# First norm per stream behind the X loads, last output banks in a fixed order, the last gate spread inside the mixer

## Chip, cores and metric

The kernel runs on one core of a Trainium2 chip. The metric is the device time of one execution in microseconds, the median of three executions. The engines of the core are TensorE (PE: matmuls, with its weight loads as PEld), VectorE (DVE), ScalarE (ACT), GpSimd (POOL) and SyncE (SP), which issues nearly all loads.

## The reference, cut to what matters

Two layers are applied to 256 latent tokens (x) and 256 context tokens (ctx), each of width 1024. The two streams share the weights and have their own shift, scale and gate (nine vectors for each layer, made from c and c_ctx).

```python
def rmsnorm(x, w):
    r = lax.rsqrt(jnp.mean(x32 * x32, axis=-1, keepdims=True) + EPS)
    return (x32 * r) * w

def trunk_layer(xl, xc, ml, mc, ...):
    xl = xl + 0.5 * g1l * swiglu(modulate(rmsnorm(xl, norm_w[0]), sh1l, sc1l), w_ffn1_in, w_ffn1_out)
    # the same for xc
    hl = modulate(rmsnorm(xl, norm_w[1]), sh2l, sc2l)        # and hc
    mix_l, mix_c = token_mixer(hl, hc, w_in, ...)            # latent attention | gated conv, one output projection
    xl = xl + g2l * mix_l
    xl = xl + 0.5 * g3l * swiglu(modulate(rmsnorm(xl, norm_w[2]), sh3l, sc3l), w_ffn2_in, w_ffn2_out)
    # the same for xc, except behind the mixer of the last layer

for i in range(DEPTH):                                       # DEPTH = 2
    ml = split(silu(c) @ w_ada[i] + b_ada[i], 9)             # and mc from c_ctx
    xl, xc = trunk_layer(...)
return rmsnorm(xl, final_norm_w)
```

The output is the latent stream, 256 x 1024 in float32.

## The kernel before, in words

**Layout.** The residual stream lies transposed in SBUF as `X`: eight tiles (`kt` or `m`, 128 features each) of 512 columns, the 256 context tokens (s = 0) first and then the 256 latent tokens (s = 1). Every float32 product is made of three matmuls (`mm3`, L224 to L226) on a high and a low part of both operands. `wload` reads a weight tile of 128 x 1024 (512 KB), makes its high part on ACT (L216) and its low part on DVE or POOL (L220). It holds three raw slots and five slots for each part. The order of the instructions on every queue is laid out when the program is built, by a scheduler that plays the program through on modelled times; the order of the Python code is only the priority. `tc.issue_after(x)` binds instructions behind `x` on their own engine.

**Start (L702 to L740).** SP loads the condition vectors, then the first pair of modulation weights (`waf`, for `ct` = 0), then `norm_w` and `b_ada`, then `X` in four pieces of 512 KB. The first norm squares the pieces on ACT (L715), sums them over four feature tiles at a time with a strided DVE reduction (L716), and calls `rstd` once for both streams: column sums on PE (`psn_s`, L239), add epsilon on DVE (L242), the power -1/2 on POOL (L244), and a spread over the partitions on PE (`psn_r`, L247), copied to `R0` by ACT (L718). Then the loop over `ct` runs. For each of the eight feature tiles it makes the shift and scale of the first norm (`ada_first`: 128x32 matmuls `psa` on `waf`, L145, copy L148; `ada_first_end`: matmuls with `sel`, L153, and three small DVE operations into `first`). It then applies the norm (`Norm.apply`: `t` on DVE L296, high part `h` on ACT L297, low part on DVE L298, for each stream), and adds this tile's share to six products of the first feed-forward layer that are kept open at once (`early`, banks `mme`). `waf` has four slots for each of its two halves.

**Modulation.** The other 128 chunks of `w_ada` are multiplied and summed on DVE (`ada_chunk`, L173) beside the feed-forward products; `PACE` says how many go with each step of a feed-forward layer, and `ada_until` fetches at once what is still missing.

**The mixer (L480 to L699)** makes the projections, the keys and queries, and goes through the heads in a software pipeline, with convolution matmuls as filler. It ends with `into_x`, which adds the output projection to `X` (L343) and squares the new tiles for the next norm (`acc`, L275 and L279). In the last layer `Norm.ahead` also makes unnormed operands (`ax`, L265 and L266), on which the next two pairs of products (`psf`) start.

**The last feed-forward layer (`ffn_end`)** keeps the latent stream alone, and its second product has tokens in the rows. Four PSUM banks (`pse`: two token tiles `tt` by two halves `h` of the features) gather it over eleven steps `j`. Beside step 0, `prepare` spreads the gate over the partitions (L412, matmuls with the identity, copied to `gb` at L419) and transposes three of the four quarters of the latent `X` (L423, copied to `xt` at L425). The fourth quarter is added by matmuls into its bank (L434). `gb` multiplies the weights of the second product (L211). Behind the last step the first token tile's banks get steps 8 to 10 and then the second's; for each bank `xt` is added (L463), squared with a row sum (L464) and multiplied with the final weight (L466); for each token tile `v` (L471), a power on POOL (L473), two scalings (L474, L475) and two output DMAs (L477) follow.

## Time and profile before

| what | value |
|---|---|
| median of the three runs | 1670.31 us (1669.78 to 1673.23) |
| profiled execution, its own time | 1671.43 us |
| span of the profiled execution | 1669.6 us |
| mean granted TensorE clock | 0.994 |
| PE busy | 1631.2 us (98% of the span) |
| PEld busy | 1394.4 us (84%) |
| DVE busy | 1052.5 us (63%) |
| ACT busy | 624.7 us (37%) |
| POOL busy | 189.8 us (11%) |
| read from HBM | 246.28 MB, 148 GB/s over the span |

The busy time of PE overlaps from one matmul to the next, so the distance of two starts is what a matmul costs: 0.23 us for 512 columns and 0.12 us for 256 at the full clock. The column `PEclk` of a table by stages is the granted clock as a share of the full one. In a timeline the first number is the start, the second the duration (of the whole group where `xN` stands), and the brackets give the idle time of the engine before it and what ended that.

### The profile page before, as it was taken

Reading aid. Unit: us, or ns where it says so; the run is one execution under the profiler, and the core shown is the slowest. Engines: PE = TensorE matmul, PEld = TensorE weight load, DVE = VectorE, ACT = ScalarE, POOL = GpSimd, SP = SyncE. Lnnn points to the kernel's source line nnn. Section 1 sums busy time; section 2 is a strip of 40 time slices with the busy share of each in tenths; the row PEclk is TensorE's granted clock in tenths of the full one; section 3 lists DMA queues with packets and bytes.
Section 4 is the critical chain, followed back from the end, with each engine's and each line's share of the span. In section 5 each row is a group of like instructions: output and inputs, shape, how many; then the busy total and the mean of one; then the engine's idle time right before and its main releaser. Section 6 shows DMA issues by size and latency. Waiting matters only on the chain.

```text
span 1669.6 us, 22712 instructions
## 1 busy us (share of the span) xinstructions
PE 1631.2 (98%) x8885; PEld 1394.4 (84%) x8885; DVE 1052.5 (63%) x1695; ACT 624.7 (37%) x1010; POOL 189.8 (11%) x159
## 2 busy tenths in 40 slices
PE   6999999999999999999999999999999999999998
PEld 5888888889877788888888888888888988989997
DVE  5677777776577476556555576654445479776665
ACT  4422222324466443321332243322322357664443
POOL 0000000023111240000000330000000421430000
PEclk9999999999999999999999999999999999989999
DMA  9465555552222125444444334544444323446553
GB/s 376 146 203 191 191 186 178 178 190 75 76 74 77 51 89 177 139 152 152 140 150 151 101 124 157 174 158 160 162 157 146 110 90 126 152 141 200 190 173 118
DMA packets 73355, 249.59 MB, mean 149 GB/s; under 512 B 8736, under 2 KB 12960, under 8 KB 73248
## 3 DMA queue, kind: packets, MB, share of 16 engines
q1 hardware_dynamic: 72960, 247.62, 44.7%
q8 instruction: 70, 1.15, 0.3%
q10 hardware_dynamic: 288, 0.52, 0.1%
q14 instruction: 37, 0.30, 0.1%
HBM read 246.28 MB, written 1.05 MB: 148 GB/s over the span
## 4 chain that ended last, share of the span: by engine, by line
PE 91%; DVE 3%; ACT 1%; issue 1%; DMA 1%; POOL 1%; SPq 0%; POOLq 0%; DVEq 0%; ACTq 0%
PE mm L224 27%; PE mm L225 27%; PE mm L226 26%; PE pse L224 1%; PE pse L225 1%; PE pse L226 1%; PE pso L659 1%; PE pst L646 1%; POOL wlo L220 1%; DVE h L298 1%; PE mme L224 1%; PE mme L226 1%; PE mme L225 1%; DVE t L296 1%; PE psn_r L247 1%
## 5 line engine op out<-in xcount | busy, mean ns | idle before, releaser
L216 ACT CAST whi<-wraw 128x1024 fp32r<-128x1024 f32 x314 | 328.1, 1048 | 793.8 <-PE mm L225 448.1
L225 PE MATMUL mm<-h,whi 128*128 128x512 f32 (+1 forms) x1648 | 582.3, 355 | 4.9 <-DVE h L298 4.9
L224 PE MATMUL mm<-h,whi 128*128 128x512 f32 (+1 forms) x1648 | 581.5, 357 | 3.3 <-ACT h L297 3.3
L226 PE MATMUL mm<-h,wlo 128*128 128x512 f32 (+1 forms) x1648 | 580.5, 354 | 0.0
L220 DVE TENSOR_TENSOR wlo<-wraw,whi 128x1024 fp32r<-128x1024 f32 x258 | 317.6, 1233 | 156.1 <-ACT whi L216 147.9
L224 PEld LDWEIGHTS mm<-h,whi 128*128 128x128 f32 x1648 | 309.5, 189 | 53.5 <-issue 7.3
L225 PEld LDWEIGHTS mm<-h,whi 128*128 128x128 f32 x1648 | 311.8, 189 | 48.6 <-DVE h L298 7.0
L226 PEld LDWEIGHTS mm<-h,wlo 128*128 128x128 f32 x1648 | 311.6, 189 | 42.8
L173 DVE SCALAR_TENSOR_TENSOR junk<-wa,scb 128x1024 f32<-128x1024 f32 x224 | 272.4, 1248 | 31.2 <-DMA wa<-in_w_ada 30.8
L220 POOL TENSOR_TENSOR wlo<-wraw,whi 128x512 fp32r<-128x512 f32 x112 | 156.4, 1421 | 1123.7 <-ACT whi L216 822.5
L225 PE MATMUL mm<-hid,whi 128*128 128x512 f32 (+1 forms) x627 | 223.1, 356 | 0.0
L226 PE MATMUL mm<-hid,wlo 128*128 128x512 f32 (+1 forms) x627 | 222.9, 355 | 0.0
L224 PE MATMUL mm<-hid,whi 128*128 128x512 f32 (+1 forms) x627 | 222.1, 356 | 0.0
L383 DVE TENSOR_TENSOR sg<-sg,mm 128x512 f32<-128x512 f32 (+1 forms) x85 | 51.9, 611 | 156.3 <-PE mm L226 145.8
L225 PEld LDWEIGHTS mm<-hid,whi 128*128 128x128 f32 x627 | 118.5, 189 | 16.8
L224 PEld LDWEIGHTS mm<-hid,whi 128*128 128x128 f32 x627 | 118.5, 189 | 16.8
L226 PEld LDWEIGHTS mm<-hid,wlo 128*128 128x128 f32 x627 | 118.5, 189 | 16.8
L343 DVE SCALAR_TENSOR_TENSOR X<-mm,mod,X 128x256 f32<-128x256 f32 x120 | 53.4, 479 | 91.1 <-PE mm L226 90.3
L211 DVE TENSOR_TENSOR wraw<-wraw,gb 128x1024 f32<-128x1024 f32 x22 | 26.9, 1225 | 52.9 <-DMA wraw<-in_f2r 52.3
L230 DVE TENSOR_TENSOR hid<-sg,hid 128x512 fp32r<-128x512 f32 (+1 forms) x88 | 56.1, 638 | 0.5 <-ACT hid L229 0.5
L279 DVE TENSOR_TENSOR acc<-acc,sq 128x256 f32<-128x256 f32 x62 | 44.9, 745 | 15.4 <-ACT sq L275 15.3
L229 ACT CAST hid<-sg 128x512 fp32r<-128x512 f32 (+1 forms) x88 | 49.4, 563 | 12.0 <-DVE sg L383 12.0
(198 smaller groups left out, 1455.3 us busy)
## 6 DMA issues: line engine op xcount, KB each, us to landing
wa<-in_w_ada SPq DMA_DIRECT2D x128, 512.0 KB, 4.2
wraw<-in_f1i SPq DMA_DIRECT2D x88, 512.0 KB, 3.3
wraw<-in_f2i SPq DMA_DIRECT2D x88, 512.0 KB, 3.4
wraw<-in_f1o SPq DMA_DIRECT2D x44, 512.0 KB, 3.3
wraw<-in_w_in SPq DMA_DIRECT2D x32, 512.0 KB, 3.3
wraw<-in_f2o SPq DMA_DIRECT2D x22, 512.0 KB, 3.3
wraw<-in_f2r SPq DMA_DIRECT2D x22, 512.0 KB, 4.3
waf<-in_w_ada SPq DMA_DIRECT2D x16, 512.0 KB, 8.0
```

The lines of the kernel that those rows point to most:

```text
L173: nc.vector.scalar_tensor_tensor(junk, wt, 1.0, scb[:, s, :], ALU.mult, ALU.mult, accum_out=md[:, s, ct:ct + 1])
L211: nc.vector.tensor_tensor(raw, raw, by, ALU.mult)
L216: nc.scalar.copy(w[0], raw)
L220: eng.tensor_tensor(w[1][:, a:a + step], raw[:, a:a + step], f32(w[0][:, a:a + step]), ALU.subtract)
L224: nc.tensor.matmul(ps, w[0], x[0], start=start, stop=False)
L225: nc.tensor.matmul(ps, w[0], x[1], start=False, stop=False)
L226: return nc.tensor.matmul(ps, w[1], x[0], start=False, stop=stop)
L229: nc.scalar.copy(hi, src)
L230: return eng.tensor_tensor(lo, src, f32(hi), ALU.subtract)
L279: nc.vector.tensor_tensor(self.acc[s], self.acc[s], sq, ALU.add)
L343: end = nc.vector.scalar_tensor_tensor(xm, pt[:, s * T - c[0]:(s + 1) * T - c[0]], mod(d, gate, s, m), xm, ALU.mult, ALU.add)
L383: nc.vector.tensor_tensor(sg, sg, ps[1], ALU.mult)
```

## The change

- **Start.** The four pieces of `X` are loaded first, then `norm_w` and `b_ada`, then the first pair of `waf`. The first norm is made for each stream by itself (`first_rstd`): the strided reduction is replaced by additions of 128x512 and 128x256 on DVE, `rstd` is called once for each stream, and `ada_first(0)` stands between the two calls. Ahead of all this PE gets 40 transposes of the identity, whose result nobody reads (`WARM`), and POOL one power of 128x4.
- **The gate of the last layer** is spread in `mixer` (`spread`), between the heads and `into_x`, and its chunks are asked for there; `PACE` of the second layer's first feed-forward goes from 1.25 to 1.4.
- **The three transposed quarters** are made at steps 4, 5 and 6 of `ffn_end` (`turn_x`) and no longer at step 0; the matmuls that add the fourth quarter move from step 0 of its bank to step 1.
- **The last banks.** The remaining matmuls of the second token tile's banks are bound behind those of the bank before them.
- `wload` gets an argument `after`, which no call uses.

```diff
--- before.py
+++ after.py
@@ -50,13 +50,14 @@
 BURST = (5.0, 4.0)
 KEYS_AT = (0, 1)
 TAIL = 3
+WARM = 40
 NAHEAD = 2
 POOLED = 512
 EARLY = 6
 LEAD = 1
 EARLY_AT = (1, 1, 2, 2, 3, 3)
 NT1 = 3
-PACE = (1.75, 1.0, 1.25, 0.9)
+PACE = (1.75, 1.0, 1.4, 0.9)
 
 
 @with_exitstack
@@ -111,6 +112,14 @@
     nc.vector.tensor_copy(sel, ident[:, 0:2])
     for j in range(1, 4):
         nc.vector.tensor_tensor(sel, sel, ident[:, 32 * j:32 * j + 2], ALU.add)
+
+    warm = small.tile([P, 4], F32, tag="r", name="warm")
+    nc.gpsimd.memset(warm, 1.0)
+    nc.gpsimd.tensor_tensor(warm, warm, mhalf, ALU.pow)
+
+    warmed = psn.tile([P, TT], F32, tag="psn", name="psw")
+    for _ in range(WARM):
+        nc.tensor.transpose(warmed[:, 0:P], ident, ident)
 
 
     c_sb = const.tile([P, NKT, 2], F32, name="c_sb")
@@ -204,7 +213,7 @@
 
     turn, share = [0, 0], [0]
 
-    def wload(src, n, tags=("whi", "wlo"), by=None):
+    def wload(src, n, tags=("whi", "wlo"), by=None, after=None):
         raw = slot("wraw", "wraw")[:, :n]
         load(raw, src)
         if by is not None:
@@ -217,7 +226,8 @@
         step = POOLED if pooled else n
         for a in range(0, n, step):
             eng = nc.gpsimd if pooled else nc.vector
-            eng.tensor_tensor(w[1][:, a:a + step], raw[:, a:a + step], f32(w[0][:, a:a + step]), ALU.subtract)
+            with tc.issue_after(after.ins) if after else nullcontext():
+                eng.tensor_tensor(w[1][:, a:a + step], raw[:, a:a + step], f32(w[0][:, a:a + step]), ALU.subtract)
         return w
 
     def mm3(ps, w, x, start, stop):
@@ -397,47 +407,49 @@
 
             into_x(d, gate, streams, lambda i: wo[d, half, i], hid, nxt if half else None, pace)
 
-    def ffn_end(d, wi, wr, gate, nrm):
+    def spread(col):
+
+        to = slot("g", "gb")
+        for h in range(2):
+            ps = mmtile((0, TT))
+            for k in range(4):
+                nc.tensor.matmul(ps[:, k * P:(k + 1) * P], col(4 * h + k).broadcast_to([P, P]), ident,
+                                 start=True, stop=True)
+            nc.scalar.copy(to[:, h * TT:(h + 1) * TT], ps)
+        return to
+
+    def ffn_end(d, wi, wr, gate, gb, nrm):
 
 
         share[0] = SHARE[0]
-        ada_until(d, gate)
         parts = [(tt, h) for tt in range(2) for h in range(2)]
-        gb = slot("g", "gb")
         fwb = slot("g", "fwb")
         load(fwb, fin_w.broadcast_to([P, D]))
         xt, acc = {}, {}
 
-        def across(ps, kt, col):
-            nc.tensor.matmul(ps, col.broadcast_to([P, P]), ident, start=True, stop=True)
-
-        def prepare():
-            for h in range(2):
-                ps = mmtile((0, TT))
-                for k in range(4):
-                    across(ps[:, k * P:(k + 1) * P], 4 * h + k, mod(d, gate, 1, 4 * h + k))
-                nc.scalar.copy(gb[:, h * TT:(h + 1) * TT], ps)
-            for (tt, h), tag in zip(parts[:-1], ("cv", "cv", "qf")):
-                ps = mmtile((0, TT))
-                for k in range(4):
-                    nc.tensor.transpose(ps[:, k * P:(k + 1) * P], X[4 * h + k][:, T + tt * P:T + (tt + 1) * P], ident)
-                xt[tt, h] = row(tag, "xt")
-                nc.scalar.copy(xt[tt, h], ps)
+        def turn_x(part, tag):
+            tt, h = part
+            ps = mmtile((0, TT))
+            for k in range(4):
+                nc.tensor.transpose(ps[:, k * P:(k + 1) * P], X[4 * h + k][:, T + tt * P:T + (tt + 1) * P], ident)
+            xt[part] = row(tag, "xt")
+            nc.scalar.copy(xt[part], ps)
 
         def gather(part, k, x, w):
             tt, h = part
             ps = acc[part]
             cs, fs = slice(T + tt * P, T + (tt + 1) * P), slice(h * TT, (h + 1) * TT)
-            mm3(ps, [v[:, cs] for v in x], [v[:, fs] for v in w], k == 0, k == NPAIR - 1)
-            if k == 0 and part not in xt:
+            end = mm3(ps, [v[:, cs] for v in x], [v[:, fs] for v in w], k == 0, k == NPAIR - 1)
+            if k == 1 and part == parts[-1]:
                 for i in range(4):
                     nc.tensor.matmul(ps[:, i * P:(i + 1) * P], X[4 * h + i][:, cs], ident, start=False, stop=False)
+            return end
 
         hid, w = {}, {}
         for j in range(NPAIR):
             hid[j], _ = gated(d, wi, j, nrm, [1])
-            if j == 0:
-                prepare()
+            if 4 <= j < 7:
+                turn_x(parts[j - 4], ("cv", "cv", "qf")[j - 4])
             if j == 1:
                 for part in parts:
                     acc[part] = psn.tile([P, TT], F32, tag="psn", name="pse")
@@ -455,8 +467,9 @@
                 for p in parts[:2]:
                     for k in range(NPAIR - TAIL, NPAIR - 1):
                         gather(p, k, hid[k], w[k])
-            for k in range(NPAIR - 1 if tt == 0 else NPAIR - TAIL, NPAIR):
-                gather(part, k, hid[k], w[k])
+            with tc.issue_after(end.ins) if tt else nullcontext():
+                for k in range(NPAIR - 1 if tt == 0 else NPAIR - TAIL, NPAIR):
+                    end = gather(part, k, hid[k], w[k])
             x = acc[part]
             if part in xt:
                 x = xt[part]
@@ -694,28 +707,39 @@
         for _ in steps:
             pass
 
+        gb = None
+        if last:
+            ada_until(d, 8)
+            gb = spread(lambda kt: mod(d, 8, 1, kt))
         ada_until(d, 5)
         order = (4, 5, 6, 7, 0, 1, 2, 3)
         into_x(d, 5, qs, lambda i: w_out[d, i], [MIX[k] for k in order], nxt)
-
-
-    ends = {}
-    for ct in range(LEAD):
-        waf, *ends[ct] = ada_first(ct)
-    nc.sync.dma_start(nw, norm_w)
-    nc.sync.dma_start(ba, b_ada)
+        return gb
+
+
+
+    R0 = row("tmp", "R0")
+
+    def first_rstd(s):
+        sums = row("pr", "sums").rearrange("p (k t) -> p k t", t=T)
+        for i in range(2):
+            sq = slot("kq", "sq0", (P, 4, T))
+            nc.scalar.activation(sq, Xall[:, 4 * i:4 * i + 4, s * T:(s + 1) * T], AF.Square)
+            nc.vector.tensor_tensor(sq[:, 0:2, :], sq[:, 0:2, :], sq[:, 2:4, :], ALU.add)
+            nc.vector.tensor_tensor(sums[:, i, :], sq[:, 0, :], sq[:, 1, :], ALU.add)
+        nc.scalar.copy(R0[:, s * T:(s + 1) * T], rstd([sums[:, i, :] for i in range(2)], D, T, "n"))
+
     for s, src in ((0, ctxT), (1, xT)):
         for a in (0, 4):
             nc.sync.dma_start(Xall[:, a:a + 4, s * T:(s + 1) * T],
                               src[a * P:(a + 4) * P, :].rearrange("(k p) t -> p k t", p=P))
-    sums = [row("pr", "sums") for _ in range(2)]
-    for s in range(2):
-        for i in range(2):
-            sq = slot("kq", "sq0", (P, 4, T))
-            nc.scalar.activation(sq, Xall[:, 4 * i:4 * i + 4, s * T:(s + 1) * T], AF.Square)
-            nc.vector.reduce_sum(sums[i][:, s * T:(s + 1) * T], sq.rearrange("p m t -> p t m"), axis=AX.X)
-    R0 = row("tmp", "R0")
-    nc.scalar.copy(R0, rstd(sums, D, TT, "n"))
+    nc.sync.dma_start(nw, norm_w)
+    nc.sync.dma_start(ba, b_ada)
+    ends = {}
+    first_rstd(0)
+    for ct in range(LEAD):
+        waf, *ends[ct] = ada_first(ct)
+    first_rstd(1)
     nrm = Norm(0, 0, [0, 1])
 
     early, at, we = [], [], []
@@ -749,10 +773,10 @@
         ffn(d, f1i, f1o, 2, prev, [0, 1], nrm, PACE[2 * d])
         qs = [1] if last else [0, 1]
         H, nrm = nrm.H, Norm(d, 2, qs)
-        mixer(d, H, last, nrm)
+        gb = mixer(d, H, last, nrm)
         prev, nrm = nrm, None if last else Norm(d + 1, 0, qs)
         if last:
-            ffn_end(d, f2i, f2r, 8, prev)
+            ffn_end(d, f2i, f2r, 8, gb, prev)
         else:
             ffn(d, f2i, f2o, 8, prev, qs, nrm, PACE[2 * d + 1])
```

## The prediction

> **What bounds the kernel now.** I read the head of the page first, then the table by stages, the timelines of the first 30 us and, for the two other places that the change touches, those around 1461 us and 1651 us. The head and the stages:
>
> ```profile
> span 1669.6 us, 22712 instructions
> PE 1631.2 (98%) x8885; PEld 1394.4 (84%) x8885; DVE 1052.5 (63%) x1695; ACT 624.7 (37%) x1010; POOL 189.8 (11%) x159
> 0.00:23.45 23.45, 9.23 (x60) 7.67 (x60) 11.10 (x18) 8.19 (x9) 2.90 (x8) 1.00 0.93 346
> 23.45:66.70 43.25, 43.19 (x384) 34.45 (x384) 23.69 (x60) 17.36 (x33) 0.00 (x0) 1.00 0.60 235
> 1661.12 0.39 PE L226 MATMUL pse<-whi,hid 128*128 128x512 f32 x1
> ```
>
> PE is busy 1631.2 of 1669.6 us. Of the 38.4 us left, 14.2 (23.45 - 9.23) lie ahead of 23.45 us and 8.1 behind the last matmul (the last row, to the end of the span). Between, PE hardly rests, so a step taken off another engine gains nothing there, and each matmul put there costs its full distance. The change can gain at the two ends, and near 1461 us, where PE waits for the last norm. At the start this chain sets the time:
>
> ```profile
> 5.17 2.30 PE L145 MATMUL psa<-waf,sc_pad 128*32 128x128 f32 x32 [5.17 <-DMA waf<-in_w_ada]
> 9.06 1.06 ACT L715 ACTIVATE sq<-X 128x1024 f32<-128x1024 f32 x1 [1.16 <-DMA X<-in_ctxT]
> 13.18 1.06 ACT L715 ACTIVATE sq<-X 128x1024 f32<-128x1024 f32 x1 [0.29 <-DMA X<-in_xT]
> 15.77 1.90 DVE sums L716
> 17.72 1.46 PE psn_s L239 x6
> 19.45 1.96 POOL r L244
> 21.45 2.08 PE psn_r L247 x8
> 24.18 0.88 DVE L296 SCALAR_TENSOR_TENSOR t<-X,first,R 128x256 f32<-128x256 f32 x2 [3.68 <-ACT R L718]
> 26.01 0.96 PE L224 MATMUL mme<-h,whi 128*128 128x512 f32 x3
> ```
>
> The first load asked for lands at 5.17 us, the pieces of X from 9.06 to 13.18 (three gaps of 1.37 us). Four reductions of 1.9 us, one rstd with a slow first power (1.96 us) and a slow spread (2.08 us) follow, and the first use of the norm is at 24.18 us. From 23.45 us on PE is full (43.19 of 43.25 us).
>
> **The change, part by part.**
>
> **Start.** X is now asked for first. Its first piece should land where the first load did, 5.2 us, and the last 3 x 1.37 us later, at 9.3 us. The price is on `waf` for ct = 0: it comes behind nw and ba (put at 0.5 us, about what SP took to issue one), two transfers at about 1.26 us each (the two later weight casts on ACT, at 14.39 and 15.64 us, are that far apart), so at 12.3 us instead of 5.2. The chain of the second stream: square 1.06 us to 10.4; the last two additions (0.68 for 128x512, a third of the first row below, and 0.41 for 128x256) to 11.5. The rows for this and for what follows:
>
> ```profile
> 1659.50 2.05 DVE L463 TENSOR_TENSOR xt<-pse,xt 128x512 f32<-128x512 f32 x3 [4.75 <-PE pse L226]
> 1459.54 0.41 DVE L279 TENSOR_TENSOR acc<-acc,sq 128x256 f32<-128x256 f32 x1
> 14.39 1.04 ACT L216 CAST whi<-wraw 128x1024 fp32r<-128x1024 f32 x1 [0.16 <-DMA wraw<-in_f1i]
> 15.64 1.04 ACT L216 CAST whi<-wraw 128x1024 fp32r<-128x1024 f32 x1 [0.20 <-DMA wraw<-in_f1i]
> 1469.49 0.69 POOL L244 TENSOR_TENSOR r<-v,mhalf 128x2 f32<-128x2 f32 x1 [4.15 <-DVE v L242]
> 1470.24 1.22 PE L247 MATMUL psn_r<-ident,r 128*128 128x128 f32 x4 [1.10 <-POOL r L244]
> 7.53 0.37 ACT L148 COPY ast<-psa 128x256 f32<-128x256 f32 x1 [3.47 <-PE psa L145]
> 7.96 1.01 PE L153 MATMUL psa<-sel,ast 128*128 128x2 f32 x4 [0.49 <-ACT ast L148]
> 9.08 0.22 DVE L154 TENSOR_SCALAR first<-psa,ba 128x2 f32<-128x2 f32 x1 [6.77 <-PE psa L153]
> ```
>
> Then psn_s 1.5, epsilon 0.2, the power 0.7 (the first call is spent beforehand; 1.96 before), the spread 1.2 at the slow clock, the copy 0.4: 15.7 us with the gaps. The modulation of ct = 0 is ready at about the same time: 12.3, half of 2.3 for the second half's `psa`, copy 0.4, `sel` 1.0, three small operations of 0.22 each, 0.7, so 15.6. If the second stream's psn_s stands behind that `psa` on PE's queue, the chain ends at 17.6. So the first use moves from 24.18 to 15.7 to 17.6 us, a gain of 6.6 to 8.5; I take the middle, 7.5. The division by streams gains little by itself, since each `mme` takes all 512 columns.
>
> All of this does not arrive at the end. Before, PE entered its full stretch behind 23.45 us of loading at 346 GB/s, 8.1 MB; now it starts at about 18 us with what has landed by then. DVE prepares a tile in 2.4 us (t 0.88, about as much for h, 0.66 for `first`) plus 1.2 for a weight's low part, while a tile brings PE only 1.4 us of `mme` at two open products, and 4.1 at six (18 x 0.23). I put the hunger of the first two tiles at 1.0 us. Net -6.5, with ends -3 (half eaten) and -9 (the better chain, no hunger and a warm PE).
>
> The 40 transposes are not on the path at either clock. A cold spread of four costs 1.22 us and one of eight 2.08, so one instruction of 128 columns costs 0.215 us cold ((2.08 - 1.22)/4) and 0.11 warm (below). Begun by about 2 us (an estimate: the identity is the first thing that POOL makes), 40 end between 6.4 and 10.6 us, and the first thing behind them, the first stream's psn_s, is wanted at about 9. I take no gain from a warm clock at 16 us, since PE has only scattered work from 10 to 16 us; if the clock held, it gains at most 2.3 us, half of the 4.5 us from the slow spread at 21.45 to the `mme` at 26.01, which run at nearly the full distance (0.28 us); I put it at 1.8.
>
> **The gate and the transposes.** This is where the change pays.
>
> ```profile
> L412 PE MATMUL mm<-ident,mod 128*128 128x128 f32 x16 | 2.2, 280 | 0.0
> 1461.39 1.50 PE L412 MATMUL mm<-ident,mod 128*128 128x128 f32 x12
> 1437.02 0.60 PE L646 MATMUL pst<-ident,pr 128*128 128x128 f32 x4
> 1466.11 0.42 ACT L275 ACTIVATE sq<-X 128x256 f32<-128x256 f32 x1 [2.00 <-DVE X L343]
> 1466.96 0.48 DVE L266 SCALAR_TENSOR_TENSOR ax<-X,mod,ax 128x256 fp32r<-128x256 f32 x1 [0.94 <-ACT ax L265]
> 1468.11 1.22 DVE L211 TENSOR_TENSOR wraw<-wraw,gb 128x1024 f32<-128x1024 f32 x1 [0.67 <-ACT gb L419]
> 1469.26 0.15 DVE L242 TENSOR_SCALAR v<-psn_s 128x2 f32<-128x2 f32 x1
> 1465.00:1468.00 3.00, 2.63 (x17) 2.40 (x16) 1.50 (x3) 1.87 (x5) 0.34 (x1) 0.70 0.59 182
> 1470.20:1476.40 6.20, 6.16 (x28) 6.17 (x29) 1.93 (x4) 3.38 (x6) 5.91 (x5) 0.50 0.28 85
> ```
>
> Now both stand in PE's wait for the norm, from 1461.4 to 1470.2 us, where they are free. A warm instruction costs (1.50 - 0.60)/8 = 0.11 us. The gate's 16 move to the end of the heads, where PE is full but for gaps of 0.3 us: +1.5 (ends 0 and 1.8). The 12 transposes move to steps 4 to 6, where PE never rests: +1.3 (ends 1.1 and 1.5). Against it stands the norm's chain: `v` waited behind the weight's multiplication by `gb` (1468.11 to 1469.33), since the gate came late; the last square was done at 1466.53, `ax` at 1467.44. With gate and transposes gone, psn_s can run at once and `v` at about 1467.5 instead of 1469.26: 1.8 us at most, 0 if DVE's order puts the multiplication into the chain elsewhere; I take -1.2. The clock is half behind that wait already (0.50 to 1476.4 us), and an emptier wait cannot make it slower; the restart costs the same.
>
> The pace: a feed-forward layer has 22 + 13 x 0.7 = 31.1 shares, so the three before the second mixer took (1.75 + 1.0 + 1.25) x 31.1 = 124.4 of the 128 chunks and left four to the mixer; with 1.4 none is left. DVE is busy 53% in that feed-forward, so they hide; without that cover they would cost 4 x 1.2 us, as one pass over 128x1024 (L211) takes. In the mixer one wait of 0.44 us of PE for DVE stood beside them:
>
> ```profile
> 1000.00:1250.00 250.00, 250.00 (x1105) 207.01 (x1104) 132.04 (x184) 66.62 (x81) 0.00 (x0) 1.00 0.48 161
> 1429.89 0.63 PE L646 MATMUL pst<-ident,pr 128*128 128x128 f32 x4 [0.44 <-DVE pr L636]
> ```
>
> I take -0.3 (ends -0.6 and +0.5).
>
> **The end.**
>
> ```profile
> 1662.28 0.58 ACT L464 ACTIVATE sqz<-pse 128x512 f32<-128x512 f32 x1
> 1662.76 0.19 ACT L464 ACTIVATION_READ_ACCUMULATOR sqz<-pse 128x1 f32 x1
> 1664.36 0.69 POOL L473 TENSOR_TENSOR r<-v,mhalf 128x1 f32<-128x1 f32 x1 [0.25 <-DVE v L471]
> 1665.08 0.72 ACT L474 ACTIVATE xt<-xt,r 128x512 f32<-128x512 f32 x1 [0.21 <-POOL r L473]
> ```
>
> The four banks are finished together, so three additions and four multiplications of 0.6 to 0.7 us queue on DVE, and the last scaling ends at 1665.80, 4.29 us behind the last matmul (1661.51). With the first token tile's banks done 4.1 us earlier (18 matmuls x 0.23), and the third 2.0 us earlier (9), DVE and ACT are free at the last matmul: square 0.58 + 0.19, `v` 0.15, power 0.69, scaling 0.72, and 0.3 for five gaps = 2.63. Gain 1.65 (ends 0.5, if PE waits once in the fixed order, and 2.3, with fewer output bytes at the end). The last 3.8 us, the output transfers, stay.
>
> **Sum.** -6.5 + 1.5 + 1.3 - 1.2 - 0.3 - 1.65 = -6.85 us. From the profiled execution's own 1671.43 us that gives 1664.6; it stands 1.1 us over the median of the runs, so I forecast 1663.5 us. A change under 0.2% (3.3 us) cannot be told from none here.
>
> **The rivals.**
>
> A, the clock holds: the transposes warm PE and the scattered work keeps it so until the first `mme`: -1.8, 1661.7 us. Against it: in 1465 to 1468 us PE was 88% busy, largely with transposes, and the clock fell to 0.50 nonetheless. [...]
>
> B, the start is fed by the loads: DMA is at 93% before 23.45 us and still full at 30 to 40 us, so the later pairs of `waf` do not land earlier, and PE waits for them where before it had a backlog. The gain of the start shrinks to under 1 us: 1663.5 + 5.5 to 6 = 1669 us, no change. For it: the loads are full already. Against it: DVE then waited 10.4 us for a `psa` that stood behind other matmuls, not for a load, and PE's work behind the last landing (about 40 us) is only a few matmuls of a tile:
>
> ```profile
> 30.00:40.00 10.00, 9.95 (x63) 7.92 (x60) 8.01 (x18) 5.02 (x8) 0.00 (x0) 1.00 1.04 414
> 49.95 0.22 DVE L154 TENSOR_SCALAR first<-psa,ba 128x2 f32<-128x2 f32 x1 [10.43 <-PE psa L153]
> ```
>
> C, slower, by lockstep on PE's queue in the start: each tile's `psa`, copy, `sel`, `first`, `t` and `h` take some 5 us in line (1.15 + 0.4 + 1.0 + 0.66 + 0.88 + 0.9). If the queue puts each tile's `mme` right behind and no older ones beside them, this is exposed at most of the eight tiles. It decides from (6.85 + 3.3)/8 = 1.3 us exposed for each tile; at 2 us for each it costs 16 - 6.85 = +9 us, 1679 us. For it: the backlog that hid this is smaller now. Against it: six products are open, and the stretch before shows none exposed.
>
> **How the numbers follow.** The forecast's case 0.63 (its own range 1659.5 to 1667), A 0.16, B 0.14, C 0.07. Faster by over 0.2% are the forecast and A: 0.79; within 0.2% is B: 0.14; slower is C: 0.07. The range leaves out C and the best of everything at once (-9 - 2.3 - 0.6 - 1.8 + 0 + 1.1 = -12.6, 1657.7 us), and takes in B: 1658.5 to 1669.3 us.
>
> **What would show it.** First `t` at 15.7 to 17.6 us and PE full from 18; the last `mme` 6.5 us earlier; the power at the start 0.7 us; the wait ahead of psn_r near the last norm longer in idle time but ending earlier; 28 instructions of 0.11 us in full stretches; 2.6 us from the last matmul to the last scaling. I am wrong if PE rests between 18 and 60 us, or if the layout of the order elsewhere changed with the start.

## The result, and the profile after

The change makes the kernel slower: 1681.55 us median (1679.71 to 1682.76, four runs) against 1670.43 us of the kernel before, run on the same chip (1669.78 to 1673.23); the ratio is 1.0062, with a 95% interval of 1.0045 to 1.008. The forecast was 1663.5 us with a range up to 1669.3, so it missed on the wrong side of no change. The profiled execution took 1679.71 us, its span is 1677.9 us.

The head of the page, and the table by stages, the last two rows of it from before:

```profile
span 1677.9 us, 22803 instructions
PE 1639.6 (98%) x8925; PEld 1399.3 (83%) x8925; DVE 1053.3 (63%) x1700; ACT 625.4 (37%) x1011; POOL 191.1 (11%) x162
```

```profile
0.00:21.99 21.99, 15.55 (x132) 14.05 (x132) 9.52 (x27) 9.79 (x14) 4.42 (x11) 0.82 0.91 348
20.00:85.00 65.00, 59.28 (x412) 45.04 (x405) 33.95 (x76) 25.44 (x43) 0.00 (x0) 0.91 0.57 208
13.50:27.00 13.50, 11.19 (x94) 8.75 (x90) 8.16 (x18) 5.75 (x10) 1.56 (x1) 0.53 1.02 417
71.00:75.50 4.50, 4.38 (x12) 3.46 (x13) 1.39 (x3) 1.95 (x4) 0.00 (x0) 0.63 0.00 0
1461.00:1483.00 22.00, 14.81 (x99) 14.31 (x98) 15.74 (x18) 7.85 (x13) 16.02 (x12) 0.77 0.40 138
```

```profile
20.00:85.00 65.00, 63.49 (x472) 51.37 (x473) 40.51 (x84) 27.20 (x46) 1.40 (x1) 1.00 0.64 238
1461.00:1483.00 22.00, 19.07 (x125) 18.27 (x124) 14.34 (x25) 14.89 (x27) 13.78 (x12) 0.77 0.38 120
```

PE's busy share is still 98%, which hides everything that follows. Between 20 and 85 us PE now rests 5.7 us (65.00 - 59.28) and is granted 0.91 of its clock; before, the same stretch held 1.5 us of rest (63.49 of 65 us busy), nearly all of it ahead of 23.45 us, at a granted clock of 1.00. The third and the fourth row of after are the stretches where the clock is low. The two clocks aren't like for like, since PE was slow at first in before as well, at a column of 1.00 (a `psa` matmul took 421 ns up to about 25.2 us and 273 ns at 25.8; see the last section); what is new is the stretch at 71 us. Around the last norm PE is busy 14.81 of 22 us, before 19.07. To see where the loss arises I follow one instruction that all kernels have, a Silu near the end of the second layer's first feed-forward. Before it and then after:

```profile
1258.33 0.58 ACT L382 ACTIVATE sg<-mm 128x512 f32<-128x512 f32 x1
```

```profile
1265.15 0.59 ACT L392 ACTIVATE sg<-mm 128x512 f32<-128x512 f32 x1
```

By then 6.8 us are lost. Ahead of it only the start and the third pace differ, and the pace makes none of it: the lag is the same at the Silu that starts at 1024.41 us in before (1031.23 in after), near the start of that layer. At the last matmul the lag is 9.5 us, at the end of the span 8.3.

The start of after, in the timelines of PE, POOL, DVE and ACT put in order of time (start, duration; in brackets the idle time before and what ended it):

```profile
1.60 7.37 PE L122 MATMUL psw<-ident 128*128 128x128 f32 x40 [1.60 <-POOL ident masks.py:199]
...
15.29 1.56 POOL L254 TENSOR_TENSOR r<-v,mhalf 128x2 f32<-128x2 f32 x1 [2.97 <-DVE v L252]
...
16.90 1.22 PE L257 MATMUL psn_r<-ident,r 128*128 128x128 f32 x4 [0.95 <-POOL r L254]
...
17.91 0.85 PE L162 MATMUL psa<-sel,ast 128*128 128x2 f32 x4
...
20.51 0.88 DVE L306 SCALAR_TENSOR_TENSOR t<-X,first,R 128x256 f32<-128x256 f32 x2
...
21.99 1.22 PE L234 MATMUL mme<-h,whi 128*128 128x512 f32 x2 [1.36 <-ACT h L307]
...
60.26 0.37 ACT L157 COPY ast<-psa 128x256 f32<-128x256 f32 x1 [1.47 <-PE psa L154]
...
68.39 0.50 PE L162 MATMUL psa<-sel,ast 128*128 128x2 f32 x4
...
69.00 0.22 DVE L163 TENSOR_SCALAR first<-psa,ba 128x2 f32<-128x2 f32 x1 [9.70 <-PE psa L162]
...
71.12 2.04 PE L234 MATMUL mme<-h,whi 128*128 128x512 f32 x6 [2.23 <-ACT h L307]
```

The last tile's `ast` is copied at 60.26 us, but the `sel` matmuls that use it (L162) run at 68.39. They waited for nothing but their turn: in PE's queue 36 open-product matmuls (`mme`) stand ahead of them and only 18 behind. DVE rests 9.70 us for them. Then `first`, `t` and `h` follow, PE rests 2.23 us with nothing left to do, and the 18 matmuls behind it start at 71.12 us, at a clock of 0.63 up to 75.5 us. In before, 54 such matmuls stood behind the last `sel`, so the same chain cost nothing; its PE timeline goes from the `sel` straight into them:

```profile
56.98 0.50 PE L153 MATMUL psa<-sel,ast 128*128 128x2 f32 x4
57.34 1.65 PE L224 MATMUL mme<-h,whi 128*128 128x512 f32 x6
```

The last tile is not all of it: of the 5.7 us of rest, 3.5 lie at earlier tiles (1.36, 0.34, 0.78, 0.56 and 0.45 us between 20 and 55 us).

The last norm, in the timelines of PE and DVE, in order of time:

```profile
1470.55 1.21 DVE L220 TENSOR_TENSOR wraw<-wraw,gb 128x1024 f32<-128x1024 f32 x1
...
1471.69 0.47 DVE L353 SCALAR_TENSOR_TENSOR X<-mm,mod,X 128x256 f32<-128x256 f32 x1
...
1474.58 0.59 PE L249 MATMUL psn_s<-mean,acc 128*128 128x1 f32 x2 [6.10 <-DVE acc L289]
...
1475.86 0.47 DVE L353 SCALAR_TENSOR_TENSOR X<-mm,mod,X 128x256 f32<-128x256 f32 x1
...
1476.89 0.58 PE L249 MATMUL psn_s<-mean,sq 128*128 128x1 f32 x2 [1.09 <-ACT sq L285]
...
1478.49 0.15 DVE L252 TENSOR_SCALAR v<-psn_s 128x2 f32<-128x2 f32 x1
```

Since `gb` is ready early, its multiplication with the weight (L220, 1.21 us) now stands ahead of the last two `X` updates in DVE's queue. Before, it stood behind the last of them (at 1468.11 us) and ahead of `v` alone:

```profile
1465.54 0.47 DVE L343 SCALAR_TENSOR_TENSOR X<-mm,mod,X 128x256 f32<-128x256 f32 x1
```

PE, with neither the gate's spread nor the transposes to do, rests 6.10 us in one piece.

The end went in the direction of the forecast, by half of its size up to the last scaling. The last matmul starts at 1670.63 and takes 0.39 us; the last scaling:

```profile
1670.63 0.39 PE L236 MATMUL pse<-whi,hid 128*128 128x512 f32 x1
1672.24 0.69 DVE L479 TENSOR_TENSOR z<-pse,fwb 128x512 f32<-128x512 f32 x1 [0.18 <-ACT sqz L477]
1673.76 0.72 ACT L487 ACTIVATE xt<-xt,r 128x512 f32<-128x512 f32 x1 [1.55 <-POOL r L486]
```

It ends 3.46 us behind the last matmul, before 4.29, and 0.4 us more is saved in the output transfers behind it.

### The profile page after: what moved, and what is told of

The parts are those of the page before. It is cut to its first block, busy times and chain, and to the rows that moved or that the text cites. A ratio compares the mean times of both kernels' runs of the same rounds, so it can differ in the third digit from the quotient of the medians.

```text
span 1677.9 us, 22803 instructions
## 1 busy us (share of the span) xinstructions
PE 1639.6 (98%) x8925; PEld 1399.3 (83%) x8925; DVE 1053.3 (63%) x1700; ACT 625.4 (37%) x1011; POOL 191.1 (11%) x162
## 3 DMA queue, kind: packets, MB, share of 16 engines
q8 instruction: 70, 1.15, 0.3%
## 4 chain that ended last, share of the span: by engine, by line
PE 91%; DVE 4%; ACT 2%; issue 1%; DMA 1%; SPq 0%; POOL 0%; POOLq 0%; DVEq 0%; ACTq 0%
PE mm L234 26%; PE mm L235 26%; PE mm L236 26%; PE pso L672 1%; DVE h L308 1%; PE pse L234 1%; PE pse L235 1%; PE pse L236 1%; PE pst L659 1%; DVE t L306 1%; PE mme L234 1%; PE mme L236 1%; PE mme L235 1%; PE pss L234 1%; PE pss L235 0%
## 5 line engine op out<-in xcount | busy, mean ns | idle before, releaser
L285 ACT ACTIVATE sq<-X 128x256 f32<-128x256 f32 x63 | 25.8, 416 | 75.5 <-DVE X L353 71.3
```

The source lines that it names most:

```text
L285: nc.scalar.activation(sq, xs, AF.Square)
```

## The experiments

Two losses had to be explained: one in the start, one at the last norm. The theories for the start: **Q**, the queue: more work at PE's head shifts the order that is laid out on modelled times, and the last tile's `sel` falls behind the open products. **W**: the transposes cost by themselves, by PE's time or by the clock. For the last norm: **H**, the gate's multiplication in DVE's queue holds up the `X` updates; **E**, the hole costs since the transposes that filled it are gone. (Rival B, the loads, is small in the traces: by 30 us 11.0 MB had been moved in after, 10.8 in before; by 40 us 14.6 and 14.96. It falls with start_nowarm below, which has the same order of loads and is faster than before.)

All results first. The two middle columns are read in the traces, against before (1258.33 us and the end of the last matmul at 1661.51 us); they come from one execution each. The kernels of one group ran on one chip, and the ratio is to before on that chip.

| kernel | shift at the Silu | shift at PE's end | median us | ratio, 95% interval |
|---|---|---|---|---|
| the change | +6.8 | +9.5 | 1681.55 | 1.0062 [1.0045, 1.008] |
| start | +8.3 | +7.2 | 1678.72 | 1.0048 [1.0032, 1.0064] |
| start_nowarm | -1.9 | -3.4 | 1667.74 | 0.9985 [0.9974, 0.9997] |
| nostart | +0.8 | +4.9 | 1673.98 | 1.0013 [1.0003, 1.0023] |
| tail | -0.3 | -0.5 | 1670.61 | 0.9999 [0.9987, 1.0011] |
| warm60 | -1.6 | -3.6 | 1669.2 | 0.9995 [0.9986, 1.0004] |
| warm_lead | +2.0 | +0.3 | 1671.93 | 1.0015 [1.0005, 1.0024] |
| nostart_hold | +0.7 | +1.75 | 1671.87 | 1.0012 [1.0003, 1.0022] |
| nostart_unturn | -0.2 | +2.0 | 1672.27 | 1.0017 [1.0007, 1.0026] |
| nowarm_late | +2.1 | +0.2 | 1671.09 | 1.0004 [0.9995, 1.0013] |
| after_lead | +2.1 | +6.05 | 1676.2 | 1.0037 [1.0023, 1.0051] |
| pace14 | +1.0 | -1.5 | 1669.22 | 0.9991 [0.9982, 1.0] |
| combo | -3.0 | -5.1 | 1665.34 | 0.9969 [0.9958, 0.998] |
| hold_unturn | 0.0 | -1.35 | 1670.7 | 1.0001 [0.9992, 1.001] |
| turnx | +1.8 | +1.0 | 1670.96 | 1.0007 [0.9997, 1.0016] |
| after_fix | -2.7 | -4.0 | 1667.66 | 0.9985 [0.9976, 0.9995] |

How far one trace can be trusted is seen in the table itself: the seven kernels that keep the start of before (tail, pace14, turnx and the nostart group) stand at -0.3 to +1.8 us at the Silu with the same start, and those that keep its second half move by 0 to -2.0 between the two columns. A difference of under 2 us in one trace says little by itself.

**Which part loses.** `start` is before with the whole new start, `start_nowarm` the same without the 40 transposes, `nostart` the change with the start of before, `tail` before with the binding of the last banks alone.

```diff
 # start_nowarm against start
-    warmed = psn.tile([P, TT], F32, tag="psn", name="psw")
-    for _ in range(WARM):
-        nc.tensor.transpose(warmed[:, 0:P], ident, ident)
 # tail against before
+            with tc.issue_after(end.ins) if tt else nullcontext():
+                for k in range(NPAIR - 1 if tt == 0 else NPAIR - TAIL, NPAIR):
+                    end = gather(part, k, hid[k], w[k])
```

> The kernel before with the whole change of the start alone (X first, norm per stream, 40 transposes, one early power). Theory Q (the order laid on PE's queue puts the last tile's sel matmuls behind 36 others, so PE rests and its clock falls): PE's queue here is the changed kernel's, so the whole of its loss at the start shows: 7 to 9 us slower, 1677 to 1680 us. Rival L (the loads of waf land too late because X goes first): the same time, so it is told apart by the next run. Rival H (the loss lies at the last norm and not at the start): within 2 us of before.

> The same start without the 40 transposes on PE (the early power on POOL stays). The loads keep their order, but the queue now has the last tile's sel ahead of 66 matmuls of the open products. Theory Q: no rest behind the last sel and a dense stretch from about 20 us on, so 4 to 7 us faster than before, 1664 to 1666 us. Rival L: still 7 us slower, since the loads are the same. Rival C (the slow clock in the first 27 us is what costs, and the transposes help against it): slower than with the transposes, 1680 us or more.

> The changed kernel with the start of before. Theory Q: what is left are the gate, the transposes at steps 4 to 6, the pace and the fixed order of the last banks: +1.5 to +2.5 at the last norm and the transposes, -1.2 at the end, -1 to -2 from the pace, so 1669 to 1672 us. Rival H: 5 us or more slower than before, 1675 us or more.

> The kernel before with nothing but the fixed order of the last banks (the second token tile's remaining matmuls bound behind the bank before). Every theory: 1.0 to 1.7 us faster, 1668.7 to 1669.4 us; the last scaling ends 2.7 to 3.1 us behind the last matmul instead of 4.3.

The new start loses 8 us; taken without its transposes it gains 2.5 (1670.43 x 0.0015), so the transposes make a difference of 11 us in the medians. The rest of the change loses about 2 us (0.0013) and ends 2 us above what was expected of it. start_nowarm is 2 us above its expectation too. The end by itself is within the scatter, so its time missed what every theory had expected (1668.7 to 1669.4 us), and its last scaling ends 3.4 us behind the last matmul, not 2.7 to 3.1; the trace does show 1.2 us less from the last matmul to the span's end (6.9 us for 8.1).

The loss is complete where the start's stage ends. The last open-product matmul starts at 69.50 us in before, 78.23 in start, 76.72 in after, 67.55 in start_nowarm, 66.75 in warm60, 71.20 in warm_lead and 70.70 in nowarm_late (the last three follow now).

**The queue or the transposes.** PE's queue can be written out from the built program. Behind the last `psa` of the start it holds, in matmuls: before 18 `mme`, the last `sel`, 54 `mme`; start 36, `sel`, 18; start_nowarm 6, `sel`, 66. With 60 transposes instead of 40 it is 18, `sel`, 54 again, as in before.

```diff
 # lines that only hand a value on are left out, here and below
 # warm60 against start
-WARM = 40
+WARM = 60
 # warm_lead against start (after_lead: the same against the whole change)
-                for k in range(at[e], ct):
-                    mm3(early[e], ...)
+                upto = ct if ct == NKT else max(at[e], ct - 1)
+                with tc.issue_after(ahead.ins) if ct >= 8 else nullcontext():   # ahead: this tile's last sel
+                    for k in range(at[e], upto):
+                        mm3(early[e], ...)
 # nowarm_late against start_nowarm
-            ada_first_end(kt, *ends[kt])
+            with tc.issue_after(behind.ins) if kt == NKT - 1 else nullcontext():   # behind: last mme of the tile before
+                ada_first_end(kt, *ends[kt])
```

> The kernel 'start' with 60 instead of 40 transposes on the identity at its head. Written out, TensorE's queue then ends its first stage with 18 open-product matmuls, the last tile's two selections, and 54 open-product matmuls (40 transposes: ... 36, the selections, 18 behind them; none: 6, the selections, 66). Theory Q (what costs is where the last tile's selections stand in the queue, not the transposes themselves): the transposes still end before the first psa can start or delay it by under 4 us, and the loss of 'start' goes: 1667 to 1672 us. Rival W (the transposes cost by themselves, by the time they hold TensorE or by what they do to the granted clock): half as many again cost half as much again, 1680 to 1684 us.

> The kernel 'start' with all its 40 transposes, and one binding more: from the last token tile on, the open products' matmuls on the newest tile stand behind that tile's... next selections, so that the last tile's selections stand ahead of 54 open-product matmuls instead of 18. Theory Q: the rests of the first mme products (5.7 us in 'after' behind 20 us) and the half clock at 71 us go, and with them most of the 8 us: 1667 to 1673 us. Rival W: within 2 us of 'start', 1677 to 1681 us.

> The kernel 'start_nowarm' (X first, norm per stream, no transposes on the identity) with one binding more: the last token tile's two selections stand behind the open products' matmuls on the tile before. TensorE's queue then ends the stage with 54 open-product matmuls, the two selections, 18 matmuls, where start_nowarm has 6, the selections, 66. Theory Q (the place of the selections is what costs, with no transpose in the kernel at all): a rest of 2 us or so ahead of the last 18 matmuls, then up to a full half-clock stretch (3.4 us more for the work in it): 2 to 7 us above start_nowarm, which ran at 0.9985 of before: 1670 to 1675 us. Rival W (the transposes cost by themselves, the order does not): within 1 us of start_nowarm, 1667 to 1668.5 us.

> The whole change with the binding of 'warm_lead' (the last tile's selections ahead of 54 of the open products' last matmuls; all 40 transposes stay). Theory Q: the start's loss goes here as it did in warm_lead (6.8 us below 'start' in their medians), and the loss at the last norm stays: 1673 to 1677 us, against 1681.55 for the whole change. Rival: the loss of the whole change lies elsewhere than in its start, and the time stays within 2 us of it.

In warm_lead's queue, as built, 36 `mme` stand behind the last `sel`, not 54, with 18 more behind the tile before it. Its edit moves more than the last tile: at every tile the matmuls on the newest one are put a tile later in the program (`upto`). So warm_lead tests the order of the whole stage at the same 40 transposes, and nowarm_late the place of the last `sel` alone: its queue is otherwise that of start_nowarm up to the end of the stage.

All four land where Q expected them. With all 40 transposes but another order, 6.8 us of start's loss go, and 5.3 us of the whole change's, each against a run on another chip. And the late `sel` makes a loss of the same kind without a single transpose: the median is 3.35 us over start_nowarm's, on another chip, with ratio intervals that just overlap (0.9995 to 0.9997), the stage ends 3.15 us later (70.70 for 67.55), and its trace shows the same rest at the same place. So the last tile alone makes about 3 of the 11 us between start and start_nowarm. First nowarm_late, PE's timeline and the table by stages, then start_nowarm:

```profile
62.44 0.50 PE L158 MATMUL psa<-sel,ast 128*128 128x2 f32 x4
65.10 1.94 PE L229 MATMUL mme<-h,whi 128*128 128x512 f32 x6 [2.16 <-ACT h L302]
```

```profile
60.00:71.00 11.00, 8.84 (x35) 7.12 (x34) 4.75 (x10) 4.40 (x7) 0.00 (x0) 0.84 0.03 6
```

```profile
52.37 0.50 PE L158 MATMUL psa<-sel,ast 128*128 128x2 f32 x4
```

```profile
60.00:71.00 11.00, 11.00 (x51) 9.09 (x50) 5.56 (x7) 5.01 (x8) 0.00 (x0) 1.00 0.26 83
20.00:85.00 65.00, 64.99 (x460) 52.31 (x453) 41.06 (x85) 27.71 (x45) 0.00 (x0) 1.00 0.65 241
```

Moved by hand to 62.44 us instead of 52.37, the selections bring back the 2.16 us of rest and a clock of 0.84; without that PE rests 0.01 us in 65. warm_lead gives 6.8 of the 11 us back, so if the two add, some 4 hang on the order of the earlier tiles. What it leaves over is warm_lead's distance to start_nowarm, 0.003 of the time or 5 us: its trace still has single rests of 1.36 and 1.15 us at 21 to 35 us, and 3.41 us at the half clock behind the second of them; its clock is at half from about 15 to 28 us as well. Whether a still better order would take that too, or the 40 transposes cost it by themselves, was not tried.

warm60 doesn't decide that. Half as many transposes again cost nothing (its median is 9.5 us under start's and 1.5 over start_nowarm's, on another chip), which is against W in its plain form. But two things differ from start at once: the order is that of before, at the earlier tiles as well, and the clock is low for 3.41 us only, at 18 to 22 us, where start has 17.06 us of it between 12 and 29.5 us. The low clock ahead of 28 us is a poor rival for the whole loss, though, since start_nowarm's `mme` matmuls were slow there too (0.43 us apart at 25.39 us, 0.23 at 28.66).

**The last norm.**

```diff
 # nostart_hold against nostart
-            nc.vector.tensor_tensor(raw, raw, by, ALU.mult)
+            with tc.issue_after(last_v[0].ins):        # behind the norm's v
+                nc.vector.tensor_tensor(raw, raw, by, ALU.mult)
 # nostart_unturn against nostart
-            if 4 <= j < 7:
-                turn_x(parts[j - 4], ("cv", "cv", "qf")[j - 4])
+            if j == 0:
+                for i in range(3):
+                    turn_x(parts[i], ("cv", "cv", "qf")[i])
 # and the matmuls of the fourth quarter back from step 1 of its bank to step 0
 # hold_unturn: both; after_fix: both in the whole change, and no transposes of the identity
 # turnx: before, with the transposes of X at steps 4 to 6 (and the fourth quarter at step 1)
```

> The kernel 'nostart' (all of the change but its start) with the gate's multiply with the bias row (1.2 us on VectorE) bound behind the last norm's v, so that VectorE's queue again has the last two X updates ahead of it, as before. Theory H (the hole at the last norm became longer because that multiply stands in the chain of X updates): 1.2 to 4 us below nostart, 1670 to 1672.5 us. Rival E (the hole is longer since the transposes that filled it were moved out): no change, 1673 to 1675 us.

> The kernel 'nostart' with the twelve transposes of X put back at the first step of the last mixer's closing loop, where they stand before the change. Theory H (the multiply in VectorE's queue makes the hole): within 1.3 us of nostart, 1672.5 to 1674.5 us. Rival E (the emptied hole costs): 3 to 5 us below nostart, 1669 to 1671 us.

> The kernel 'nostart' with both: the gate's multiply held behind the last norm's v (as in nostart_hold) and the twelve transposes of X back at the first step of the closing loop (as in nostart_unturn). What is left of the change is the gate spread in the mixer, the third pace and the last banks' order. nostart took 5.0 us more than before at the end of TensorE's work, nostart_hold 1.75, nostart_unturn 2.0. If multiply and transposes each cost their own part, the two together give 1.5 us below before, as pace14 has it alone: 1668 to 1669.5 us, and the gate spread is free once its multiply is held. If the sixteen products of the spread, taken out of the hole into full work, cost 2 us themselves, as their 2.2 us in the hole before say: 1670 to 1671.5 us.

> The kernel before with the twelve transposes of X moved alone, from the first step of the closing loop to its steps 4 to 6. The prediction's price is +1.3 us (12 steps of 0.11 us in full work). If the emptied hole costs no more than that: 1671 to 1672 us against 1670.4 of before, at the edge of what the times resolve; if the hole's clock turns on them: 1673 to 1675 us. The trace decides: the end of TensorE's work against 1661.5 us.

In the traces each undoing takes about 3 us off the end of PE's work (1.0 of nostart_unturn's ahead of the Silu already), and in nostart_hold the queue does what H says: the last two `X` updates come in step again, and `v` runs at 1468.56 where nostart had it at 1473.17. Counted from the mixer's first `X` update, `v` comes at 25.7 us in after, nostart and nostart_unturn, at 22.1 and 22.0 in nostart_hold and hold_unturn, and at 20.6 in before. So the multiplication alone moves `v`, by 3.6 us, with the transposes back or not: for the norm's chain H is shown, and what X's transposes cost lies behind `v`. DVE's timelines, nostart first:

```profile
1465.23 1.21 DVE L213 TENSOR_TENSOR wraw<-wraw,gb 128x1024 f32<-128x1024 f32 x1
1470.53 0.47 DVE L346 SCALAR_TENSOR_TENSOR X<-mm,mod,X 128x256 f32<-128x256 f32 x1
1473.17 0.14 DVE L245 TENSOR_SCALAR v<-psn_s 128x2 f32<-128x2 f32 x1
```

```profile
1466.04 0.48 DVE L349 SCALAR_TENSOR_TENSOR X<-mm,mod,X 128x256 f32<-128x256 f32 x1
1468.56 0.16 DVE L248 TENSOR_SCALAR v<-psn_s 128x2 f32<-128x2 f32 x1 [0.62 <-PE psn_s L245]
1468.73 1.23 DVE L214 TENSOR_TENSOR wraw<-wraw,gb 128x1024 f32<-128x1024 f32 x1
```

The times do not bear out either one alone: nostart_hold has 1.0012 and nostart_unturn 1.0017, where nostart has 1.0013. A part of the reason is in nostart_hold's trace: held right behind `v`, the multiplication (1468.73 to 1469.96 us on DVE) runs beside the power on POOL, which takes 1.72 us (from 1468.80) where nostart's takes 0.70, so 1.0 us is lost again behind `v`. Only both together bring the time down, to 1.0001, and then the end of PE's work is 1.35 us ahead of before, as pace14 has it (-1.5). So the loss belongs to the two together, about 2 us in the times, 6 in the traces, and a part of the 6 is the clock: behind the norm's wait it is at half speed for 10.24 us in before and nostart, and for 6.83 in hold_unturn. How the time divides is not settled. hold_unturn's time (1670.7 us) lies where a price of the spread was expected, its trace where none was. turnx shows that the move of X's transposes alone costs about 1 us (interval -0.5 to +2.7), which is not told from zero.

**What pays.** combo is start_nowarm with the third pace and the binding of the last banks, with gate and transposes as before.

```diff
 # pace14 against before (combo: the same in start_nowarm, with the binding of tail)
-PACE = (1.75, 1.0, 1.25, 0.9)
+PACE = (1.75, 1.0, 1.4, 0.9)
```

> The kernel before with only the third pace changed from 1.25 to 1.4. The traces of after and nostart have 1.9 us less than before between the last Exp but a few and the first X update of the last mixer; if the pace makes that, this kernel is 1 to 2 us faster, 1668 to 1669.5 us; if the gate's part there makes it, it stays within 0.5 us of before.

> The parts that paid in the traces, together: X first and the norm per stream without the transposes on the identity (-3.4 us at the end of TensorE's work in start_nowarm), the last banks issued tile by tile (-1.2 us from the last matmul to the span's end in 'tail'), the third pace at 1.4; gate and X's transposes as before. If the parts add: 1664 to 1666.5 us, 0.9965 to 0.998 of before. If the length of the half-clock stretches decides from run to run, the gain is smaller, 1667 to 1669 us.

> The whole change mended in the three places: no transposes on the identity, the gate's multiply held behind the last norm's v, X's transposes at the first step of the closing loop. If the three are the whole loss, it is as fast as combo (0.9969 of before): 1664 to 1666.5 us. If the gate spread costs by itself, it stays 1.5 to 2.5 us above combo: 1667 to 1668.5 us.

combo beats both kernels: 1665.34 us, 0.9969 of before (0.9958 to 0.998) and 16 us under the change, on another chip. after_fix, which is the whole change with its three faults mended, has 0.9985: the three are the whole loss against before and more. It stays 0.0016 of the time or 2.7 us above combo, which does without the gate spread (the intervals overlap by 0.0004); in the traces 1.1 us. That isn't the price of the spread alone: the held multiplication runs beside the power here too, which takes 1.72 us for 0.70 in combo.

## Why the prediction was wrong, step by step

**Start, forecast -6.5, measured +8.3 in `start`'s trace and +8.0 in the times: the step that failed.** The loads came as worked out (squares at 5.21, 6.72, 8.13 and 9.52 us in after). Three things were wrong behind them.

1. "I put the hunger of the first two tiles at 1.0 us." I priced a chain of engines as if the order on PE's queue stayed; it was laid out anew, and the last tile's turn came too late. This is what rival C described (a tile's `psa`, copy, `sel`, `first`, `t`, `h` exposed), with its sign, but not at every tile: the rests add up to 5.7 us (1.5 in before), 2.23 of them at the last tile, and the low clock behind it costs up to 2 us more (4.5 us at 0.63). That C's 1679 us came near is partly luck, since it has no loss at the last norm and 2 us at each of eight tiles. I gave it 0.07, on the ground that "six products are open"; what counts is how many of their matmuls stand behind the `sel`, 54 in before and 18 in after.
2. "The 40 transposes are not on the path at either clock." True of their time (they end at 8.97 us, `psn_s` starts at 8.81 behind them), wrong for the kernel: on the modelled times they move the order (the queues of start and start_nowarm differ from the first tiles on). My own closing sentence named it, "if the layout of the order elsewhere changed with the start", but it had no term and no chance of its own.
3. Without the transposes the start still gains only 2 to 3 us. The first `t` came at 20.51 us in after, where 15.7 to 17.6 was forecast: the second stream's `psn_s` had its sums at about 11.7 us and ran at 13.59, behind the first stream's spread and half of `psa` in PE's queue, the second power took 1.56 us, not 0.7, and a weight's low part of 1.22 us came between two of the small operations into `first`. That an early first power saves 1.26 us was, it seems, a misreading: the second power, though not the first call any more, began while DVE made a low part (15.07 to 16.29 us) and ended at 16.85, 0.56 us behind it. So did the 1.72 us of nostart_hold, 0.56 us behind the multiplication. In before a low part ran beside the 1.95 us as well (19.28 to 20.51; the power ended at 21.40, 0.89 us behind it), so a first call need not have made them. Whether the power waits for such an operation was not tried by itself. And what came earlier ran slowly. In start_nowarm the first `mme` run 0.43 us apart:

```profile
21.81 1.65 PE L229 MATMUL mme<-h,whi 128*128 128x512 f32 x3
25.39 0.63 PE L231 MATMUL mme<-h,wlo 128*128 128x512 f32 x1
25.82 0.63 PE L230 MATMUL mme<-h,whi 128*128 128x512 f32 x1
28.89 0.40 PE L229 MATMUL mme<-h,whi 128*128 128x512 f32 x1
29.12 0.39 PE L230 MATMUL mme<-h,whi 128*128 128x512 f32 x1
```

The step is 0.43 us at 25.4 and 0.23 at 28.9; in before it is 0.23 from about 26.8 us on, too. So the 4.2 us by which the first `mme` came forward (21.81 for 26.01) were worked at about half speed (0.43 us for 0.23), and at the last `mme` 1.95 are left (67.55 for 69.50).

**Rival A** had its first half right: PE sped up on the transposes alone. All 40 of them, which the built program marks as transposes, then those behind 7 us, in the view of their tile:

```profile
L122 PE MATMUL psw<-ident x40: 272/421/476, 1.6 to 8.7; 128*128 128x128 f32 x40
L122 PE MATMUL psw<-ident x16: 272/273/421, 6.8 to 8.7; 128*128 128x128 f32 x16
```

One takes 421 ns at first and 273 ns from about 7 us on, and from 1.60 to 8.81 us PE had nothing else to do. The second half failed: the scattered work behind them did not keep the clock, which was granted at 0.53 on average from 13.5 to 27 us. The first `mme` came no earlier for it (21.99 us, 21.81 in start_nowarm).

**Gate and transposes, forecast +1.5 + 1.3 - 1.2 = +1.6; with the pace and the end nostart lost about 2 us in the times where -0.35 was forecast.** The gate's own price of 1.5 is not contradicted (after_fix above combo by 1.1 us in the traces and 2.7 in the times, the longer power included), and X's transposes cost about 1 us alone (turnx), for 1.3. The term that failed is the norm's chain: "0 if DVE's order puts the multiplication into the chain elsewhere; I take -1.2". DVE's order did put it elsewhere, ahead of two `X` updates, and then it is a loss, since each later square, `acc` and `psn_s` waits; the end of 0 should have stood above zero. `v` came 25.7 us behind the first of the mixer's `X` updates in after (1478.49 and 1452.80 us), 20.6 in before (1469.26 and 1448.64). Where the multiplication stays behind, the forecast gain is there: in turnx `v` came at 19.0 us (1469.32 and 1450.28), 1.6 us sooner.

**Pace, forecast -0.3, measured -1.2 us (pace14, interval -3.0 to 0).** Sign right, size too small; the trace has 2.0 us less from the Silu to the mixer's first `X` update.

**The end, forecast -1.65.** The trace gives -0.83 to the last scaling and -0.4 in the transfers; the time of `tail` alone cannot tell it from zero. 2.63 us from the last matmul became 3.46: the multiplication into `z`, 0.69 us, stands ahead of `v` on DVE (1672.24 and 1672.85 us), and my sum has no term for it.

## What to carry to other kernels

Where the order of the queues is laid out from modelled times, work that is off the path on the chip can still move what is on it: compare the written-out queue of the new kernel with the old one at the places where a chain over several engines comes back to PE, and count how many matmuls stand behind the instruction that starts the chain. Work that was free in a hole may cost time elsewhere (turnx: about 1 us for the twelve transposes, within the scatter). An operand that becomes ready earlier may be used earlier, perhaps ahead of what everybody waits for, as the gate's multiplication was here (1470.55 us in after, the `X` updates at 1471.69 and 1475.86); bind it behind the chain. And a start that is pulled ahead on a TensorE that is slow at first (`mme` 0.43 us apart for 0.23) gained here about half of what the chain shows (1.95 of 4.2 us).

## What the runs showed of the hardware that I had not expected

The granted clock as the page has it does not show the first slow stretch: it reads 1.00 in start_nowarm while matmuls of 512 columns are 0.43 us apart, and in before while 32 `psa` matmuls take 2.30 us (at 5.17 us) that take 1.08 later (at 48.23 us). In after the first 0.50 stands from about 14 to 28 us, behind the transposes that took 273 ns. In the first slow stretch the distance of two starts is the measure.

The half-clock stretch at the last norm has different lengths in kernels with the same code there. The 60 us from 1440 to 1500, in the tables by stages of before, start and start_nowarm:

```profile
1440.00:1500.00 60.00, 56.77 (x415) 54.21 (x412) 42.55 (x65) 34.83 (x66) 30.42 (x23) 0.91 0.44 141
```

```profile
1440.00:1500.00 60.00, 55.68 (x427) 52.55 (x426) 42.75 (x75) 35.77 (x70) 31.18 (x24) 0.94 0.40 128
```

```profile
1440.00:1500.00 60.00, 56.00 (x427) 53.92 (x427) 45.05 (x65) 34.87 (x63) 28.71 (x22) 0.97 0.45 150
```

Granted clocks of 0.91, 0.94 and 0.97 are about 10, 7 and 3.5 us at half speed ((1 - 0.91) x 60 / 0.5 = 10.8, and so on). Added up over windows of half a microsecond they are 10.24, 6.83 and 3.41 us, so three, two and one times 3.41; and the stretches in the starts are such multiples too, 13.66 and 3.41 us in after, 17.06 and 3.41 in start (the two have the same code there, and their stages end 1.5 us apart). The lowest value of the half-microsecond windows of before and after is 0.50. No run shows what sets these lengths. 10.24 us at half speed instead of 3.41 are 3.4 us of lost time ((10.24 - 3.41) / 2, an estimate), near the 4 us by which one kernel's runs scatter; whether that is why they scatter was not tried by itself.
